# Rooms for down's operands during up, groups of 4, 4, 3 and 3 pairs, and the second norm's plain copy on VectorE, in an encoder step on one Trainium2 core

## The chip, the cores and the metric

The kernel runs on one core of one Trainium2 chip. The metric is the device time of one execution in microseconds (us). The engines are TensorE (PE in the profile; PEld is its weight load), VectorE (DVE), ScalarE (ACT), GpSimd (POOL) and SyncE (SP); SP issues nearly all DMAs here, one after the other, in the order that was fixed when the kernel was built.

## The reference

The reference is one step of a two-layer encoder over 1024 prompt tokens and 32 sample tokens (1056 together), with model width 1024 and hidden width 4096. Layer 0 mixes tokens with an mLSTM, layer 1 with attention over a band of chunks; each is followed by an MLP with a squared ReLU, and each half ends in a layer norm. The change touches the second half of layer 1, and the norm ahead of it:

```
x = layer_norm(ALPHA * x + (1 + g1) * y, ln_g[l, 0], ln_b[l, 0])
u = x * (1 + sc2) + sh2
f = square(relu(u @ w_up[l])) @ w_down[l]
x = layer_norm(ALPHA * x + (1 + g2) * f, ln_g[l, 1], ln_b[l, 1])
```

Everything is float32. A product of matrices is made of three matmuls on operands split into a high and a low part: high by high, high by low, low by high.

## The kernel before

`split` (L88 to L90) makes the two parts of an operand: ACT copies the value into a rounded type (L89, the high part), VectorE subtracts that from the value (L90, the low part). A weight block passes through a landing tile of the tag `raw` (three buffers in a ring pool), is split into a tile of the tag `wc` (six buffers), and is then read by TensorE. Buffers of a tag are handed out in the order in which the program asks for them.

The norm ahead of the MLP (L826 to L891) runs over three token blocks, last one first. For each it subtracts the mean (L844, L857), squares (L859), sums (L844 again), makes the factor (L869 to L874), multiplies (L876), and calls `modulate` (L324) for eight feature chunks and one or two stretches of tokens. `modulate` makes the input u of the MLP: ACT writes its high part (L326), a plain float32 copy of u is made by the engine that is named in the call (here ACT, L330; without a name VectorE, L328), and VectorE subtracts the one from the other (L331). The norm's steps lie between other work by a small planner (`flow`), which advances its generators as matmuls are written.

Layer 1's MLP works on four quarters of 264 tokens (`QN`), and on 16 pairs of 128 hidden features' blocks, 256 features in each. Quarters 3 and 2 are token half 1, quarters 1 and 0 are token half 0, and half 1 comes first. *Up* computes, for a pair and a half, four tiles of 24 matmuls (L118 to L120). For pairs 0 to 13 the four results are squared and combined into seven matrices of a seven-product scheme for blocked multiplication, split, and written to device memory (`hd`, L1468) by groups of pairs (`GRP`: 3, 4, 4 and 3). Pairs 14 and 15 are plain: their squares are split and written to `hpl` (L1473). They are the last of up: pairs 14 and 15 of half 1, then 14 and 15 of half 0.

*Down* then runs over units. A unit is a group and one of four pairs of output blocks; in a unit each token half takes seven products, each of 12 matmuls in a group of 4 pairs and 9 in a group of 3 (L1568). The weights of a unit are two blocks `rdn` (L1518), from which seven combined and split forms `wf` are made by ACT and VectorE (L1535 to L1538, L89, L90) while the unit before runs. The seven operands `fx` of each half are loaded from `hd` (L1551) into fourteen rooms; each is reloaded for the next group as soon as the last unit of the old group has used it. VectorE adds every product to the residual (ACC, L963). The order of the matmuls in down is written out by hand.

The rooms before: one tile of its own (f1), eight in the space that u holds during up (two for each quarter of u), four in a pool (f4) that takes the space of up's combining tiles H and HL after the last pair, and one `wc` tile. The first unit of the first group is split in two, so that output blocks 0 of half 1 and blocks 1 come before blocks 0 of half 0. At the end the plain pairs are read back (`hs`), multiplied with their part of the weights in four token blocks, and the last norm writes the result.

Of the kernel before, what the change touches and what calls it, by code (L numbers as in the profile page):

```python
# [15 lines left out]
P = 128  # L16
# [59 lines left out]
def trunk_kernel(ctx: ExitStack, tc: tile.TileContext, a, o):  # L76
# [744 lines left out]
    def make_layer(acc, pp, uo, usegs=segs):  # L821
# [4 lines left out]
        def norm(ti, ni, nm, w, affine=True, after=None):  # L826
# [48 lines left out]
            for i in range(0, KC, 2):  # L875
                nc.vector.tensor_mul(x[:, i:i + 2], x[:, i:i + 2], w2[:, 0:1].broadcast_to([P, 2, n]))  # L876
                for k in (i, i + 1):
                    for off, m, cnd in usegs(t0, n):
                        tmp = tmp_t([P, 384], f"ut_{nm}_{k}_{off}")
                        modulate(x[:, k, off:off + m], m, comb[:, ni, k, 0, cnd:cnd + 1],  # L880
                                 comb[:, ni, k, 1, cnd:cnd + 1], uo(0, k, t0 + off, m), uo(1, k, t0 + off, m),
                                 tmp[:, :m], nc.scalar)
                if i < 6:
                    yield w[2 + i // 2]
# [175 lines left out]
        return mm, norm, norm_out, out_proj, mlp, gain_shift, add_gated_at  # L1060

# [320 lines left out]

    QN = T // 4
# [41 lines left out]

    NPB, KG = 16, 4
    GRP = [(0, 3), (3, 4), (7, 4), (11, 3)]  # L1430
    NW = 14
    B11, B22, B21, T1, T3, T2, T4 = range(7)
    hd = [[dr.tile([7, P, 2, kg, QN], F32, name=f"hd_{g}_{tp}") for tp in range(2)] for g, (_, kg) in enumerate(GRP)]
    hpl = dr.tile([4, P, 2, T], F32, name="hpl")
    f1_cm = tc.tile_pool(name="f1", bufs=1, reuse_waits="tile")
    f1p = f1_cm.__enter__()
    hh_cm = tc.tile_pool(name="hh", bufs=1, reuse_waits="tile")
    hhp = hh_cm.__enter__()
    w_up, w_dn = a["w_up"][1], a["w_down"][1]
    wups, hts = {}, {}  # L1440

    def up_w(pb):
        if pb not in wups:
            wups[pb] = [wblock(f"up1_{pb}_{i}", w_up, 512 * i, pb * 256) for i in range(2)]
        return wups[pb]

    def up_tile(pb, f, q):

        tp = q // 2
        ps = mm(f"up1_{pb}_{f}_{q}")  # L1450
        proj(ps[:, :QN], QN, up_w(pb), f, lambda hl, k: u2[q][:, hl, k])
        if (pb, tp) not in hts:
            hts[pb, tp] = [hhp.tile([P, 8, QN], F32, tag="H", name=f"H_{pb}_{tp}", bufs=2), 0]
        H = hts[pb, tp][0]
        nc.scalar.activation(H[:, ((0, 1), (3, 2) if pb < NW else (2, 3))[f][q % 2]], ps[:, :QN], AF.Relu)
        hts[pb, tp][1] += 1
        if hts[pb, tp][1] == 4:
            nc.scalar.activation(H[:, 0:4], H[:, 0:4], AF.Square)
            HL = hhp.tile([P, 2, 7, QN], F32R, tag="HL", name=f"HL_{pb}_{tp}", bufs=1)
            if pb < NW:  # L1460
                nc.vector.tensor_sub(H[:, 4:6], H[:, 1:3], H[:, 0:2])
                nc.vector.tensor_sub(H[:, 6], H[:, 2], H[:, 4])
                nc.vector.tensor_sub(H[:, 7], H[:, 3], H[:, 6])
                split(HL[:, 0, 0], HL[:, 1, 0], H[:, 0])
                split(HL[:, 0, 1:], HL[:, 1, 1:], H[:, 2:])
                g = [i for i, (p0, kg) in enumerate(GRP) if p0 <= pb][-1]
                for hl in range(2):
                    nc.sync.dma_start(hd[g][tp][:, :, hl, pb - GRP[g][0]].rearrange("f p t -> p f t"),  # L1468
                                      HL[:, hl].bitcast(F32))
            else:  # L1470
                split(HL[:, 0, 0:4], HL[:, 1, 0:4], H[:, 0:4])
                for c in range(2):
                    nc.sync.dma_start(hpl[2 * (pb - NW) + c, :, :, 2 * tp * QN:2 * (tp + 1) * QN],  # L1473
                                      HL[:, :, 2 * c:2 * c + 2].bitcast(F32).rearrange("p l q t -> p l (q t)"))
        flow.tick(QN / 96)

    def up_unit(pb, tp):
        for f in range(2):
            for q in (2 * tp, 2 * tp + 1):
                up_tile(pb, f, q)  # L1480


    for pb in range(2):
        up_w(pb)
    flow.finish(norms[2])
    for pb in range(2):
        for f in range(2):
            up_tile(pb, f, 3)
    flow.finish(norms[1])
    for pb in range(2):  # L1490
        for f in range(2):
            up_tile(pb, f, 2)
    up_unit(2, 1)
    flow.finish(norms[0])
    for pb in range(3):
        up_unit(pb, 0)
    for pb in range(3, NPB - 2):
        for tp in (1, 0):
            up_unit(pb, tp)
    for tp in (1, 0):  # L1500
        for pb in (NPB - 2, NPB - 1):
            up_unit(pb, tp)

    PRODS = [(0, B11, 0), (1, B21, 1), (2, T2, 0), (3, T1, 2), (4, T3, 0), (5, B22, 2), (6, T4, 0)]
    gate1 = ada_part(1, 5)  # L1510

    def forms(g, m, nm):

        raw = []
        p0, kg = GRP[g]
        for i in range(2):
            r = raw_tile([P, kg, 256], f"rdn_{nm}_{i}")
            nc.sync.dma_start(r, w_dn[p0 * 256:(p0 + kg) * 256, m * 256:(m + 1) * 256].rearrange(  # L1518
                "(k s p) c -> s p k c", s=2, p=P)[i])
            raw.append(r)  # L1520
        out = []

        def pair():
            w = ring.tile([P, 2, 2, kg, P], F32R, tag="wc", name=f"wf_{nm}_{len(out)}", bufs=6)
            out.extend([w[:, 0], w[:, 1]])
            return w
        yield out
        a11, a21 = raw[0][:, :, 0:P], raw[0][:, :, P:256]
        a12, a22 = raw[1][:, :, 0:P], raw[1][:, :, P:256]
        w = pair()  # L1530
        split(w[:, 0, 0], w[:, 0, 1], a11)
        split(w[:, 1, 0], w[:, 1, 1], a12)
        yield out
        s1, s2, s3, s4 = (tmp_t([P, kg, P], f"s{i}_{nm}") for i in range(4))
        nc.vector.tensor_add(s1, a21, a22)  # L1535
        nc.vector.tensor_sub(s2, s1, a11)
        nc.vector.tensor_sub(s3, a11, a21)
        nc.vector.tensor_sub(s4, a12, s2)  # L1538
        for x, y in ((s2, s1), (s3, s4)):
            w = pair()  # L1540
            split(w[:, 0, 0], w[:, 0, 1], x)
            split(w[:, 1, 0], w[:, 1, 1], y)
            yield out
        w = pair()
        split(w[:, 0, 0], w[:, 0, 1], a22)
        yield out

    fx = {}

    def load_f(g, tp, f):  # L1550
        nc.sync.dma_start(fx[tp, f][:, :, :GRP[g][1]].bitcast(F32), hd[g][tp][f])  # L1551

    def unit(g, m, phases, ws, step, after):


        kg = GRP[g][1]
        for tps in phases:
            ps = {}
            for i, (w, f, b) in enumerate(PRODS):
                for tp in tps:  # L1560
                    first = (tp, b) not in ps
                    if first:
                        ps[tp, b] = mm(f"dn1_{g}_{m}_{tp}_{b}")
                    p = ps[tp, b][:, :QN]
                    x = fx[tp, f]
                    for k in range(kg):
                        for n_, (wl, xl) in enumerate(((0, 0), (0, 1), (1, 0))):
                            nc.tensor.matmul(p, ws[w][:, wl, k], x[:, xl, k], start=first and k + n_ == 0,  # L1568
                                             stop=k == kg - 1 and n_ == 2, skip_group_check=not first)
                    c, q = ((0, 0), (0, 0), (0, 1), (1, 1), (1, 1), (0, 1), (1, 0))[i]  # L1570
                    add_gated_at((2 * tp + q) * QN, QN, p, gate1, 2 * m + c)
                    after(tp, f)
                if tps is phases[-1]:
                    step(i)


    def u2_room(q):
        t = u2p[q].tile([P, 2, 2, KG, QN], F32R, tag="u2", name=f"fx_{q}")
        return [t[:, 0], t[:, 1]]
    order_f = [f for _, f, _ in PRODS]  # L1580
    preps, ready = {}, {}
    units = [(0, 0, [(1,)]), (0, 1, [(1,), (0,)]), (0, 0, [(0,)]), (0, 2, [(1, 0)]), (0, 3, [(1,), (0,)])]
    for g in range(1, len(GRP)):
        units += [(g, m, [(1,), (0,)] if m in (0, 3) else [(1, 0)]) for m in range(4)]

    def prep(i):
        if i < len(units):
            preps[i] = forms(*units[i][:2], f"{i}")
            next(preps[i])
    room = u2_room(3) + u2_room(2) + [f1p.tile([P, 2, KG, QN], F32R, name="fx_1")]  # L1590
    for f in order_f[:5]:
        fx[1, f] = room.pop(0)
        load_f(0, 1, f)
    prep(0)
    for _ in range(4):
        ready[0] = next(preps[0])
# [89 lines left out]
```

## Time and profile before

| what | value |
|---|---|
| median of 3 runs | 2502.86 us (2498.45 to 2505.21) |
| profiled execution | 2503.12 us |
| its span, first to last instruction | 2501.3 us |
| mean granted TensorE clock | 0.991 |
| busy: TensorE, VectorE, ScalarE, GpSimd | 2418.5, 1755.0, 1040.4, 167.4 us |
| second norm with the start of up | about 1704 to 1790 us |
| up of layer 1 to its end | to 2113.9 us |
| down by products | 2113.9 to about 2420 us |

The times of the trace are counted from the first instruction of the profiled execution. A row of windows gives from:to, the length, PE's busy time and its number of matmuls, the granted clock (1.00 is full speed), the share in which DMA engines were busy, and GB/s. A row of waits gives the waiting engine, tile and line, what it waited for, the sum in us, how many times, and the longest. A row of groups gives line, engine, operation and shapes, then busy time, mean ns of one, and the idle time ahead of them with what ended it.

### The profile page before, as it was taken

The numbers are of one execution on the slowest core, as the hardware profiler recorded it, in microseconds if no ns is written. First come the engines' busy times: TensorE is split into PE (matmuls) and PEld (weight loads), VectorE is DVE, ScalarE is ACT, GpSimd is POOL, SyncE is SP. The second block draws the span as 40 slices with busy tenths as digits, with TensorE's granted clock in tenths as the row PEclk, the third lists the DMA queues.
The fourth block names the chain that finished last, engine by engine and source line by source line (L and its number), as shares of the span: only waits on it lengthen the run. The fifth ranks groups of instructions, "written<-read, shape, count | busy, mean of one in ns | idle before, by whom it ended". The sixth has DMA issues, their size and how long they took to land.

```text
span 2501.3 us, 42666 instructions
## 1 busy us (share of the span) xinstructions
PE 2418.5 (97%) x16844; PEld 2315.5 (93%) x16844; DVE 1755.0 (70%) x4033; ACT 1040.4 (42%) x2185; POOL 167.4 (7%) x315
## 2 busy tenths in 40 slices
PE   7999999999999999999999899998999999989997
PEld 4999999999999999999999877798999999889997
DVE  4899998778778768766696667737644442766678
ACT  4644455481221221221375566737944443211122
POOL 0211100000000000000001144400000000000003
PEclk9999999999999999999999999999999999999999
DMA  8433234313324323333123400051486667567552
GB/s 295 120 109 100 84 90 132 98 35 118 92 87 126 93 90 121 93 93 115 59 89 94 107 1 2 18 146 43 149 261 209 213 200 247 179 239 285 185 177 70
DMA packets 256108, 316.78 MB, mean 127 GB/s; under 512 B 11160, under 2 KB 233516, under 8 KB 251812
## 3 DMA queue, kind: packets, MB, share of 16 engines
q1 hardware_dynamic: 255908, 314.07, 38.7%
q8 instruction: 132, 2.16, 0.4%
q14 instruction: 68, 0.56, 0.1%
HBM read 241.48 MB, written 74.91 MB: 126 GB/s over the span
## 4 chain that ended last, share of the span: by engine, by line
PE 78%; DVE 7%; DMA 6%; ACT 3%; issue 1%; POOL 0%; SPq 0%; DVEq 0%; ACTq 0%; POOLq 0%
PE up L118 10%; PE up L119 10%; PE up L120 10%; PE dn L1568 8%; PE dn L119 5%; PE dn L118 5%; PE dn L120 5%; PE pv L1308 2%; PE pt L1288 2%; PE s L1258 2%; DMA fx_w<-hd 2%; DMA fx<-hd 1%; PE o L118 1%; PE o L119 1%; PE o L120 1%
## 5 line engine op out<-in xcount | busy, mean ns | idle before, releaser
L1568 PE MATMUL dn<-fx,wf 128*128 128x264 f32 x2184 | 276.7, 286 | 21.0 <-DMA fx<-hd 12.7
L1568 PEld LDWEIGHTS dn<-fx,wf 128*128 128x128 f32 x2184 | 270.4, 190 | 25.8 <-issue 10.9
L119 PE MATMUL up<-u,w_up 128*128 128x264 f32 x1024 | 290.8, 285 | 0.6 <-DVE u L331 0.6
L120 PE MATMUL up<-u,w_up 128*128 128x264 f32 x1024 | 290.0, 285 | 0.0
L118 PE MATMUL up<-u,w_up 128*128 128x264 f32 x1024 | 289.1, 286 | 0.2 <-ACT w_up L89 0.2
L119 PE MATMUL dn<-h,w_dn 128*128 128x384 f32 (+1 forms) x768 | 249.5, 325 | 0.0
L118 PE MATMUL up<-U,w_up 128*128 128x384 f32 (+1 forms) x768 | 249.2, 324 | 0.0
L119 PE MATMUL up<-U,w_up 128*128 128x384 f32 (+1 forms) x768 | 247.9, 323 | 0.0
L118 PE MATMUL dn<-h,w_dn 128*128 128x384 f32 (+1 forms) x768 | 247.8, 323 | 0.0
L120 PE MATMUL up<-U,w_up 128*128 128x384 f32 (+1 forms) x768 | 247.6, 322 | 0.0
L120 PE MATMUL dn<-h,w_dn 128*128 128x384 f32 (+1 forms) x768 | 247.3, 322 | 0.0
L963 DVE SCALAR_TENSOR_TENSOR ACC<-dn,ada,ACC 128x264 f32<-128x264 f32 (+5 forms) x328 | 133.1, 427 | 105.5 <-PE dn L1568 96.6
L119 PEld LDWEIGHTS up<-u,w_up 128*128 128x128 f32 x1024 | 194.5, 190 | 1.1 <-DVE u L331 1.1
L118 PEld LDWEIGHTS up<-u,w_up 128*128 128x128 f32 x1024 | 193.4, 190 | 0.6 <-ACT w_up L89 0.6
L120 PEld LDWEIGHTS up<-u,w_up 128*128 128x128 f32 x1024 | 193.3, 189 | 0.3 <-DVE w_up L90 0.3
L238 DVE SCALAR_TENSOR_TENSOR aacc<-rada,cs,aacc 128x256 f32<-128x256 f32 x448 | 190.3, 477 | 0.0
L963 DVE SCALAR_TENSOR_TENSOR acc<-dn,ada,acc 128x384 f32<-128x384 f32 (+2 forms) x256 | 119.3, 486 | 47.0 <-PE dn L120 45.9
L1000 ACT ACTIVATE r<-up 128x384 f32<-128x384 f32 (+1 forms) x96 | 44.2, 462 | 244.5 <-PE up L120 236.7
L119 PEld LDWEIGHTS dn<-h,w_dn 128*128 128x128 f32 x768 | 144.5, 188 | 0.2 <-DVE h L1003 0.2
L120 PEld LDWEIGHTS dn<-h,w_dn 128*128 128x128 f32 x768 | 144.5, 188 | 0.0
L120 PEld LDWEIGHTS up<-U,w_up 128*128 128x128 f32 x768 | 144.3, 188 | 0.0
L118 PEld LDWEIGHTS up<-U,w_up 128*128 128x128 f32 x768 | 144.2, 188 | 0.1
(350 smaller groups left out, 5986.6 us busy)
## 6 DMA issues: line engine op xcount, KB each, us to landing
hd<-HL SPq DMA_DIRECT2D x56, 924.0 KB
rada<-in_w_ada_dram SPq DMA_DIRECT2D x64, 512.0 KB
raw_up<-in_w_up_dram SPq DMA_DIRECT2D x64, 512.0 KB
fx<-hd SPq DMA_DIRECT2D x26, 1056.0 KB
fx<-hd SPq DMA_DIRECT2D x26, 792.0 KB
raw_dn<-in_w_down_dram SPq DMA_DIRECT2D x36, 512.0 KB
ada_room<-in_w_ada_dram SPq DMA_DIRECT2D x32, 512.0 KB
rada<-in_w_ada_kv_dram SPq DMA_DIRECT2D x16, 512.0 KB
```

Source lines behind the costliest of these rows:

```text
L118: nc.tensor.matmul(ps, wh, mov(0, k), start=(k == 0), stop=False)
L119: nc.tensor.matmul(ps, wh, mov(1, k), start=False, stop=False)
L120: nc.tensor.matmul(ps, wl, mov(0, k), start=False, stop=(k == nk - 1))
L238: nc.vector.scalar_tensor_tensor(acc[:, cnd], raw[:, k], sc, acc[:, cnd], op0=ALU.mult, op1=ALU.add)
L963: nc.vector.scalar_tensor_tensor(xs, ps[:, off + o:off + o + mm_], gate[:, fc, cnd:cnd + 1], xs, op0=ALU.mult, op1=ALU.add)
L1000: nc.scalar.activation(r, ps[:, :n], AF.Relu)
L1258: nc.tensor.matmul(s[:, b, :w], qst, kk[i][:, g, k0 + j0:k0 + j0 + w], start=(i == 0), stop=(i == 1))
L1288: nc.tensor.transpose(pt[:kp, j - j0, pr * P:(pr + 1) * P], ps_[pr][:, j * P:j * P + kp], ident)
L1308: nc.tensor.matmul(pv[64 * e:64 * e + 64, :nq], V[:kp, vt0 + j, g * 64:(g + 1) * 64], pts[e][:kp, j, :nq], start=(j == 0), stop=(j == nt - 1))
L1568: nc.tensor.matmul(p, ws[w][:, wl, k], x[:, xl, k], start=first and k + n_ == 0, stop=k == kg - 1 and n_ == 2, skip_group_check=not first)
```

## The change

The whole of layer 1's MLP moves into a function (`mlp7`) with a small class for what is the layer's own. Beside that:

- The groups are 4, 4, 3 and 3 pairs. The first unit is no longer split, so there are 16 units and not 17.
- The pool of H and HL is closed before the plain pairs, and f4 opens there. The plain pairs get a function of their own, `up_plain`: ACT applies the ReLU into a temporary, VectorE squares it, and it is split into a tile hl, which is taken from the tag `raw` and stored to `hpl`, one store for each feature block and half.
- f1 and the four f4 rooms take the first five operands and are filled before the plain pairs. The rooms in u's quarters 3 and 2 are filled after the plain pairs of half 1, where also the weights of the first unit are requested (`prep(0)`); those in quarters 1 and 0, and the `wc` tile, after the plain pairs of half 0.
- At the end, `hs` takes the f4 tiles, and the last norm's gain and bias take a tile in u's quarter 3.
- In the norm of layer 1 that feeds the MLP, `modulate` is called without an engine, so VectorE makes the plain copy. Layer 0 keeps ACT.

```diff
-                                 tmp[:, :m], nc.scalar)
+                                 tmp[:, :m], nc.scalar if usegs is segs else None)
...
-    GRP = [(0, 3), (3, 4), (7, 4), (11, 3)]
+    GRP = [(0, 4), (4, 4), (8, 3), (11, 3)]
...
+        def up_plain(pb, tp):
+            for f in range(2):
+                r = tmp_t([P, 2, QN], f"hr{l}_{pb}_{f}_{tp}")
+                for i in range(2):
+                    nc.scalar.activation(r[:, i], up_mm(pb, f, 2 * tp + i), AF.Relu)
+                    flow.tick(QN / 96)
+                nc.vector.tensor_mul(r, r, r)
+                hl = ring.tile([P, 2, 2, QN], F32R, tag="raw", name=f"hl{l}_{pb}_{f}_{tp}", bufs=3)
+                split(hl[:, 0], hl[:, 1], r)
+                nc.sync.dma_start(hpl[2 * (pb - NW) + f, :, :, 2 * tp * QN:2 * (tp + 1) * QN],
+                                  hl.bitcast(F32).rearrange("p l q t -> p l (q t)"))
...
+        hh_cm.__exit__(None, None, None)
+        f4_cm = tc.tile_pool(name=f"f4{l}", bufs=1, reuse_waits="tile")
+        f4p = f4_cm.__enter__()
...
-    units = [(0, 0, [(1,)]), (0, 1, [(1,), (0,)]), (0, 0, [(0,)]), (0, 2, [(1, 0)]), (0, 3, [(1,), (0,)])]
-    for g in range(1, len(GRP)):
-        units += [(g, m, [(1,), (0,)] if m in (0, 3) else [(1, 0)]) for m in range(4)]
+        units = [(g, m, [(tp0,), (tp1,)] if m in (0, 3) else [(tp0, tp1)]) for g in range(len(GRP)) for m in range(4)]
...
+        f4 = [f4p.tile([P, 2, KG, QN], F32R, tag=f"f4{i}", name=f"fx_4{i}_{l}") for i in range(4)]
+        rooms = [Room(t) for t in [f1p.tile([P, 2, KG, QN], F32R, name=f"fx_1_{l}")] + f4]
+        want = [(tp, f) for tp in L.pairs for f in order_f]
+
+        def fill(new):
+            for r in new:
+                tp, f = want.pop(0)
+                fx[tp, f] = r
+                load_f(0, tp, f)
+        fill(rooms)
+        for tp in L.pairs:
+            for pb in range(NW, NPB):
+                up_plain(pb, tp)
+            if tp == tp0:
+                fill(L.rooms(tp0))
+                prep(0)
+        for _ in range(4):
+            got[0] = next(preps[0])
+        fill(L.rooms(tp1))
+        fill([Room(ring.tile([P, 2, KG, QN], F32R, tag="wc", name=f"fx_w{l}", bufs=6))])
...
-    hs = [t[:, i] for q in (3, 2) for t in [u2p[q].tile([P, 2, 2, T], F32R, tag="u2", name=f"hs_{q}")] for i in range(2)]
+        hs = [f4p.tile([P, 2, T], F32R, tag=f"f4{c}", name=f"hs_{l}_{c}") for c in range(4)]
...
-    gb = f4p.tile([P, 2, D], F32, tag="f40", name="gb")
+            L1.gb = u2p[3].tile([P, 2, D], F32, tag="u2", name="gb")
```

Here `L.pairs` is (1, 0), so `tp0` is half 1, the half that comes first, and `L.rooms(h)` gives the four rooms in the two quarters of half h.

More of the change, by code (lines that the diff above doesn't have):

```diff
@@ L1060, in make_layer, with __init__, mov, load @@
         return mm, norm, norm_out, out_proj, mlp, gain_shift, add_gated_at
+    QN = T // 4
+    NPB, KG = 16, 4
+    NW = 14
+    GRP = [(0, 4), (4, 4), (8, 3), (11, 3)]
+    B11, B22, B21, T1, T3, T2, T4 = range(7)
+    PRODS = [(0, B11, 0, 0, 0), (1, B21, 1, 0, 0), (2, T2, 0, 0, 1), (3, T1, 2, 1, 1), (4, T3, 0, 1, 1),
+             (5, B22, 2, 0, 1), (6, T4, 0, 1, 0)]
+    class Room:
+        def __init__(self, t, pieces=None):
+            self.t, self.pieces = t, pieces
+        def mov(self, hl, k):
+            return self.t[:, hl, k] if self.pieces is None else self.pieces(hl, k // 2)[:, k % 2 * QN:(k % 2 + 1) * QN]
+        def load(self, src, kg):
+            if self.pieces is None:
+                nc.sync.dma_start(self.t[:, :, :kg].bitcast(F32), src)
+                return
+            for hl in range(2):
+                for k in range(0, kg, 2):
+                    n = min(2, kg - k)
+                    nc.sync.dma_start(self.pieces(hl, k // 2)[:, :n * QN].bitcast(F32),
+                                      src[:, hl, k:k + n].rearrange("p k t -> p (k t)"))
@@ L1381, in trunk_kernel @@
         more_wo(ti)
-    QN = T // 4
     u2_cm, u2p, u2 = [], {}, {}
@@ L1424, in trunk_kernel @@
     out_proj([(0,), (1, 2, 3)], rev, wo_get, o_mov, ada_part(1, 2), end_out1, "b", width=[384, 384, 320])
-    NPB, KG = 16, 4
-    GRP = [(0, 3), (3, 4), (7, 4), (11, 3)]
[L1431 to L1574, printed above, removed]
@@ L1577, in u2_room @@
[L1577 to L1581, printed above, removed]
-    units = [(0, 0, [(1,)]), (0, 1, [(1,), (0,)]), (0, 0, [(0,)]), (0, 2, [(1, 0)]), (0, 3, [(1,), (0,)])]
-    for g in range(1, len(GRP)):
-        units += [(g, m, [(1,), (0,)] if m in (0, 3) else [(1, 0)]) for m in range(4)]
[L1586 to L1596, printed above, removed]
-    hh_cm.__exit__(None, None, None)
-    f4_cm = tc.tile_pool(name="f4", bufs=1, reuse_waits="tile")
-    f4p = f4_cm.__enter__()
-    room = u2_room(1) + u2_room(0) + [f4p.tile([P, 2, KG, QN], F32R, tag=f"f4{i}", name=f"fx_4{i}") for i in range(4)]
-    room.append(ring.tile([P, 2, KG, QN], F32R, tag="wc", name="fx_w", bufs=6))
@@ L1602, in trunk_kernel @@
-    for tp, fs in ((1, order_f[5:]), (0, order_f)):
-        for f in fs:
-            fx[tp, f] = room.pop(0)
-            load_f(0, tp, f)
-    with tc.manual_schedule(engines={mybir.EngineType.PE}):
-        for i, (g, m, phases) in enumerate(units):
-            prep(i + 1)
-            def step(j):
-                if i + 1 in preps and j in (0, 1, 3, 5):
-                    ready[i + 1] = next(preps[i + 1])
-            def after(tp, f):
-                if m == 3 and g + 1 < len(GRP):
-                    load_f(g + 1, tp, f)
-            unit(g, m, phases, ready[i], step, after)
@@ L1620, in trunk_kernel @@
-    hs = [t[:, i] for q in (3, 2) for t in [u2p[q].tile([P, 2, 2, T], F32R, tag="u2", name=f"hs_{q}")] for i in range(2)]
-    for c in range(4):
-        nc.sync.dma_start(hs[c].bitcast(F32), hpl[c])
-    ybuf = [t[:, i] for q in (1, 0) for t in [u2p[q].tile([P, 4, D], F32, tag="u2", name=f"yb_{q}")] for i in range(4)]
-    gb = f4p.tile([P, 2, D], F32, tag="f40", name="gb")
-    nc.sync.dma_start(gb[:, 0], a["ln_g"][1, 1:2].broadcast_to([P, D]))
-    nc.sync.dma_start(gb[:, 1], a["ln_b"][1, 1:2].broadcast_to([P, D]))
@@ L1628, in put_out, with u, ready, rooms @@
-    def put_out(t, m, yr, hf):
-        for off, n, cnd in segs(t, m):
-            dst = o["y_sample"][0] if cnd else o["y_prompt"][0, t:t + n]
-            nc.sync.dma_start(dst[:, 512 * hf:512 * hf + 512], yr[off:off + n, 512 * hf:512 * hf + 512])
-    ws = [wblock(f"dn1_{pr}", w_dn, NW * 256, pr * 256) for pr in range(4)]
-    ny = [0]
-    def next_y(name):
-        ny[0] += 1
-        return ybuf[(ny[0] - 1) % 8]
-    for t0, n in ((0, 288), (288, 256), (544, 256), (800, 256)):
-        for fc in range(KC):
-            ps = mm(f"dn1_{fc}_{t0}")
-            proj(ps[:, :n], n, [ws[fc // 2]], fc % 2, lambda hl, k: hs[k][:, hl, t0:t0 + n])
-            add_gated_at(t0, n, ps, gate1, fc)
-            flow.tick(n / 192)
-        tiles = [(t, min(P, t0 + n - t)) for t in range(t0, t0 + n, P)]
-        flow.add(norm_out(tiles, put_out, next_y, gb, t0 == 800), TAIL[0])
+    class L1:
+        l, alloc, add, gate = 1, mm, add_gated_at, ada_part(1, 5)
+        order, blocks = rev, [(0, 288), (288, 256), (544, 256), (800, 256)]
+        pairs, quarters = (1, 0), (3, 2, 1, 0)
+        def u(hl, k, q):
+            return u2[q][:, hl, k]
+        def ready(i):
+            flow.finish(norms[rev[i]])
+        def rooms(pr):
+            out = []
+            for q in (2 * pr + 1, 2 * pr):
+                t = u2p[q].tile([P, 2, 2, KG, QN], F32R, tag="u2", name=f"fx_{q}")
+                out += [Room(t[:, i]) for i in range(2)]
+            return out
+        def end(f4p):
+            L1.ybuf = [t[:, i] for q in (1, 0) for t in [u2p[q].tile([P, 4, D], F32, tag="u2", name=f"yb_{q}")]
+                       for i in range(4)]
+            L1.gb = u2p[3].tile([P, 2, D], F32, tag="u2", name="gb")
+            nc.sync.dma_start(L1.gb[:, 0], a["ln_g"][1, 1:2].broadcast_to([P, D]))
+            nc.sync.dma_start(L1.gb[:, 1], a["ln_b"][1, 1:2].broadcast_to([P, D]))
+            L1.ny = 0
+        def put_out(t, m, yr, hf):
+            for off, n, cnd in segs(t, m):
+                dst = o["y_sample"][0, t + off - TP:t + off - TP + n] if cnd else o["y_prompt"][0, t:t + n]
+                nc.sync.dma_start(dst[:, 512 * hf:512 * hf + 512], yr[off:off + n, 512 * hf:512 * hf + 512])
+        def next_y(name):
+            L1.ny += 1
+            return L1.ybuf[(L1.ny - 1) % 8]
+        def after(blk):
+            t0, n = blk
+            tiles = [(t, min(P, t0 + n - t)) for t in range(t0, t0 + n, P)]
+            flow.add(norm_out(tiles, L1.put_out, L1.next_y, L1.gb, blk == L1.blocks[-1]), TAIL[0])
@@ L1646, in trunk_kernel @@
+    mlp7(L1)
     flow.finish()
     psD_cm.__exit__(None, None, None)
-    f4_cm.__exit__(None, None, None)
-    f1_cm.__exit__(None, None, None)
     for cm in reversed(u2_cm):
```

145 lines of the change are left out of this document (added).

## The prediction

> **What bounds the kernel now.** I read the page's engine shares first, then windows of layer 1's MLP, then TensorE's waits, then the chain of waits between up and down.
>
> ```profile
> span 2501.3 us, 42666 instructions
> ...
> PE 2418.5 (97%) x16844; PEld 2315.5 (93%) x16844; DVE 1755.0 (70%) x4033; ACT 1040.4 (42%) x2185; POOL 167.4 (7%) x315
> ...
> hd<-HL SPq DMA_DIRECT2D x56, 924.0 KB
> ...
> raw_up<-in_w_up_dram SPq DMA_DIRECT2D x64, 512.0 KB
> fx<-hd SPq DMA_DIRECT2D x26, 1056.0 KB
> fx<-hd SPq DMA_DIRECT2D x26, 792.0 KB
> ```
>
> TensorE (PE) is busy 97% of the span, and the change leaves the number of matmuls as it is. So only stretches in which PE doesn't run at its pace can move the time. Windows of PE (from:to, length, busy and matmuls, granted clock, DMA):
>
> ```profile
> 1728.00:1790.00 62.00, 55.02 (x400) 0.92 0.36 113
> 1790.00:2060.00 270.00, 270.00 (x2236) 1.00 0.68 222
> 2060.00:2113.60 53.60, 53.60 (x445) 1.00 0.61 211
> 2113.60:2160.00 46.40, 36.05 (x258) 0.89 0.61 219
> 2196.00:2240.00 44.00, 35.82 (x277) 1.00 0.64 244
> 2296.00:2310.00 14.00, 11.04 (x85) 1.00 0.89 339
> 2346.00:2350.00 4.00, 4.00 (x35) 1.00 0.32 102
> ```
>
> Undisturbed up runs 2236 matmuls in 270.00 us, 0.1208 us each; a tile of 24 takes 2.90 us, four tiles 11.6. Length less matmuls times 0.1208 is what a window loses: 13.7 us in the second norm (1728 to 1790), nothing in the rest of up, plain pairs included, 15.2 between up and down (2113.6 to 2160), 10.5 where a group of 3 pairs gives way to one of 4 (2196 to 2240), 3.7 from 4 to 4 (2296 to 2310), nothing from 4 to 3 (2346 to 2350).
>
> ```profile
> PE dn L1568 <- DMA fx<-hd: 12.7, 11, 5.1
> ...
> PE mean_n L844 <- ACT sr_n L89: 3.3, 2, 3.2
> PE var_n L844 <- ACT qr_n L89: 3.0, 1, 3.0
> ...
> PE dn L1568 <- DMA fx_w<-hd: 1.9, 2, 0.9
> ```
>
> The largest wait is for fx, down's operands. The chain in order of time (start, length, what):
>
> ```profile
> 2113.76 0.13 PE up L120
> 2113.92 0.40 ACT H L1455
> 2114.34 1.10 ACT H L1458
> 2115.46 1.08 ACT HL L89
> 2116.57 1.26 DVE HL L90
> ...
> 2118.46 0.61 SPq L1473
> 2119.12 7.73 DMA fx<-hd
> ...
> 2126.99 2.33 PE dn L1568 x9
> ...
> 2130.33 7.81 DMA rdn<-in_w_down_dram
> ...
> 2141.93 3.46 DMA rdn<-in_w_down_dram
> ```
>
> Operands that need room freed by up are requested only behind the last plain store, at 2119.12, and PE stands for them. An rdn load (384 KB) issued at 2130.33, behind these loads, lands after 7.81 us; the same load at 2141.93 takes 3.46. SP's loads are served in order, and a late place in its queue is paid in full. By the Trainium skill (DMA: Bandwidth & Descriptors, "Queues, rings and completion order") one sequencer's DMAs share one row of rings, each consumed in ring order; the two rdn rows agree.
>
> **The change part by part.** *Room before the plain pairs: the transition.* Five of the first seven operands are requested before the plain pairs' products, four more after the first half's plain pairs, five after the last. Seven products of 12 matmuls last 84 x 0.1208 = 10.1 us, so unit 0 (both halves) covers 20.3 us of arrivals. After up's end SP still sends five operands (1056 KB), three plain stores and unit 1's two weight blocks of 512 KB.
>
> ```profile
> GB/s 0 288 346 313 181 24 0 349 345 252 0 0 331 218 65 366 398 350 394 278 309 11 119 134 393 91 192 420 341 379 388 242 412 410 401 399 398 376 229 8
> ...
> hpl<-HL SPq DMA_DIRECT2D x8, 528.0 KB
> ```
>
> A backed-up queue moves about 405 GB/s (this is the rate in 2060 to 2140, in 40 slices). Those 7,888 KB take 19.9 us, plus the 2.5 us that the free rdn load took beyond its 0.97 us of data: 22.4, plus a cast and subtraction of some 1.3: 23.7 against 20.3 covered. Remainder about 3 us; of 15.2 are saved 12. If the cover fails, the whole 15.2 comes back.
>
> *Groups 4, 4, 3, 3.* A new group's 14 operands are requested one by one as the 14 products of the old group's last unit end, and read in turn by the 14 of the new one's first. Count from the start of that last unit: products are 1.45 us (12 matmuls) in a group of 4 and 1.09 (9) in one of 3, operands at 405 GB/s (the row of rates below) 2.67 and 2.00, the next units' weights 2.6 and 1.9, and 2.5 us pass in an unhurried load beside its data. From 3 to 4 the 14th lands at 1.09 + 14 x 2.67 + 2.5 + 2.6 = 43.6 and is wanted at 14 x 1.09 + 13 x 1.45 = 34.1: lost 9.5, against 10.5 measured. From 4 to 4: 43.9 and 39.1, lost 4.8 (measured 3.7). From 4 to 3: 33.9 and 34.4, none, as measured. From 3 to 3, which is new: 33.5 and 29.3, lost 4. New sum 3.7 + 0 + 4 = 7.7, old 14.2: saved 6.5. One unit's weight forms fewer lie beside PE; nothing.
>
> *What is put ahead of pair 15's weights.* The plain pairs now write hl tiles of the tag "raw", three buffers, the tag of the weights' landing tiles. In the built order, SP issues raw_up_15 only behind the store of pair 14's second hl tile, and that behind pair 13's last stores, the first hl store and four operand loads; before, pair 15's weights stand ahead of all these, and 2060 to 2113.6 shows no wait. ACT's and VectorE's casts for pair 15 follow the same way.
>
> ```profile
> L1468 SPq DMA_DIRECT2D hd<-HL x2: 360/360/360, 2073.1 to 2075.0; - x2
> ```
> ```profile
> L90 DVE TENSOR_TENSOR w_up<-raw_up,w_up 128x1024 fp32r<-128x1024 f32 x26 | 31.4, 1222 | 21.9 <-ACT w_up L89 21.9
> ...
> L89 ACT CAST w_up<-raw_up 128x1024 fp32r<-128x1024 f32 x26 | 27.2, 1046 | 7.8 <-PE up L120 7.2 <-DMA raw_up<-in_w_up_dram 0.5
> ...
> L1461 DVE TENSOR_TENSOR H<-H 128x528 f32<-128x528 f32 x25 | 17.6, 705 | 42.5 <-ACT H L1458 42.5
> ```
>
> Up ends at 2113.9, 16 tiles after pair 13: call that moment A = 2113.9 - 46.4 = 2067.5. PE wants pair 15 at A + 11.6. Free of any queue: relu 0.40, square 0.71, copy about 0.6 (between nothing and 1.08 for twice the size), subtraction 0.71, store's issue 0.61, so the weights go out near A + 14.7, land 3.8 later (3.46 plus 128 KB more), and cast and subtraction (1.05 + 1.22) end at A + 20.8: PE stands 9.2 us. With the queue: from pair 13's first store (2073.1, A + 5.6) lie ahead 2 x 924, 528, 4 x 1056, 528 and the block's own 512 KB, 7.82 MB, 19.3 us; with 2.5 and the casts A + 29.7: PE stands 18.1. I take the queue's value, since the rows of the transition show this queue in order and backed up. And the clock afterwards:
>
> ```profile
> 2118.50:2127.00 8.50, 2.65 (x19) 0.82 1.00 359
> 2127.00:2134.20 7.20, 6.59 (x28) 0.50 1.03 402
> ```
>
> After the 5 us wait PE had half its clock for about 7 us, 6.59 busy, 3.3 lost. Taken likewise: 18.1 + 3.3 = 21.4. By the Trainium skill (TensorE: Matmul & The Clock Gate, "What's actually happening") a busy window of about 3.4 us brings the clock back, which would lose 1.7; the row here is longer, and I keep 3.3.
>
> The removed squares (one of 1056 on ACT per half pair, now VectorE's) lie beside up's matmuls: nothing.
>
> *The norm's plain copy on VectorE.*
>
> ```profile
> 1704.00:1790.00 86.00, 78.60 (x535) 76.01 (x534) 66.88 (x125) 78.70 (x167) 0.00 (x0) 0.94 0.26 82
> ```
> ```profile
> L330 ACT ACTIVATE ut_n<-ACC,comb 128x240 f32<-128x240 f32 x8 | 4.6, 575 | 0.0
> ...
> L330 ACT ACTIVATE ut_n<-ACC,comb 128x24 f32<-128x24 f32 x8 | 3.1, 392 | 0.0
> ```
> ```profile
> L328 DVE TENSOR_SCALAR utmp<-xt,ada x32: 296/445/480, 36.0 to 63.1; 128x384 f32<-128x384 f32 x16, 128x256 f32<-128x256 f32 x8, 128x32 f32<-128x32 f32 x8
> ```
>
> Busy here, in the order PE, PEld, DVE, ACT: ACT 78.70 of 86, VectorE 66.88. The copies (first and last of seven groups shown) cost ACT 0.39 to 0.58 us each, 56 of them some 27; layer 0's same operation costs VectorE 0.30 to 0.48, at the norm's widths of 24 to 264 some 18 for 56 (an estimate from that row). VectorE would have 85 of 86 us, so the bound changes hands and the stage can't shrink much. Bounds: half of the 13.7 lost gone (the waits for ACT's sr_n and qr_n, 6.3, are its part), or the 18 us pushing the last sums 4 later. I take +1, near the VectorE sum.
>
> *Sum.* 21.4 - 12 - 6.5 + 1 = +3.9 on the profiled 2503.1 (span 2501.3 and 1.8 around it, 0.3 above the median): 2507, less that 0.3. I give 2506.
>
> **Rivals.** *The weights aren't held by the queue* (faster): loads of several requests share the engines, and pair 15's small blocks land in about 3.8 us. For it: in the built order PE interleaves three tiles' first matmuls at pair 15, a short wait for the low halves. Against: the two rdn rows. The wait is then 9.2 and little clock is lost: 2506 - 12 = 2494. It decides once the blocks land before A + 21.
> *The transition keeps its stall* (slower): SP stands until up's end at a load into the last quarters' room, with three stores, four loads and rdn behind it; landings 12 us later than worked out (a slower queue, or hl tiles that wait for their stores) bring the 12 us back: 2518. It decides where unit 1's first block lands later than 25 us after up's end. Against: 20.3 us of cover.
> *ACT's relief shortens the norm* (within the bound): the 6.3 of waits go: 2499. Against: VectorE's 85 of 86. The opposite, VectorE 8 late: 2513.
>
> **How the numbers follow.** A change under 0.3%, 7.5 us, can't be told from none. Forecast 0.46 (2499 to 2513, 0.36 of it within the bound, 0.10 above); weights early 0.20 (0.18 faster, 0.02 within); transition stall kept 0.16, slower; norm shorter 0.10 (0.05 faster with a shorter clock loss, 0.05 within); VectorE late 0.08, slower. Faster 0.23, same 0.43, slower 0.34. Range 2492 (weights early) to 2519 (stall kept).
>
> **What would show it.** Right: a PE wait of some 18 us at pair 15's first tile for w_up and raw_up, with half clock behind it, and SP's raw_up after four fx loads; up's end 20 us later; at most 3 us between up and down, ended by rdn or its forms; losses of about 4 at the first and the third group change; VectorE near full between 1704 and 1790. Wrong: pair 15 starting without a wait, fx waits after up's end, or a norm window that moves by more than 6 us.

## The result, and the profile after

| | before | after |
|---|---|---|
| median of 16 runs | 2503.66 us (2497.53 to 2508.17) | 2509.74 us (2503.0 to 2515.06) |
| profiled execution, its span | 2503.12 us, 2501.3 us | 2513.09 us, 2511.3 us |

The ratio is 1.0027, with a 95% interval of 1.0017 to 1.0036: 6 us slower by the medians, which is under the 0.3% that was named as the limit of what can be told from no change, though the interval excludes 1. The forecast was 2506 us.

The profiled execution of after is 10.0 us longer than that of before, and 3 us above its own median. 2.4 us of this lie ahead of everything that was changed: the norm's first mean starts at 1688.8 in the one and at 1691.2 in the other, before the first plain copy in either (1706.1 and 1708.7), and over the thirteen kernels of this study that moment scatters between 1686.9 and 1691.5. The rest is read from windows that answer to those shown of before (from:to, length, PE busy and matmuls, granted clock, DMA share, GB/s):

```profile
1728.00:1794.00 66.00, 54.71 (x404) 0.95 0.35 111
1794.00:2060.00 266.00, 266.00 (x2202) 1.00 0.66 215
2060.00:2139.50 79.50, 60.85 (x489) 0.89 0.64 226
2139.50:2186.00 46.50, 43.58 (x352) 1.00 0.62 222
2236.00:2250.00 14.00, 11.20 (x88) 1.00 0.96 375
2320.00:2330.00 10.00, 9.64 (x78) 1.00 0.74 261
2380.00:2396.00 16.00, 12.72 (x97) 1.00 0.92 343
2084.20:2102.80 18.60, 0.04 (x1) 0.64 0.94 342
2102.80:2106.80 4.00, 3.91 (x17) 0.53 0.00 0
```

With 0.1208 us to a matmul, as in the prediction, the losses are:

| place | before | after | change |
|---|---|---|---|
| second norm | 13.7 | 17.2 | +3.5 |
| plain pairs, to up's end | 0 | 20.4 | +20.4 |
| behind up's end | 15.2 | 4.0 | -11.2 |
| group changes | 10.5 + 3.7 + 0 | 3.4 + 0.6 + 4.3 | -5.9 |
| sum | | | +6.8 |

Two rows depend on where their windows begin and end. The norm's windows both begin at 1728, where the profiled execution of after is 2.4 us late; counted from the same matmul to the same matmul (the norm's first mean to the 401st of up, 102.0 and 104.8 us) the norm takes 2.8 us more. A group change also loses a little outside the short windows. Counted from the start of the old group's last unit to the end of the new group's second, the three changes lose 11.3, 4.0 and 0.8 us before and 3.8, 1.6 and 5.7 after, 5.0 less; the last of them, from 3 pairs to 3, is

```profile
2358.18:2409.93 51.75, 47.95 (x381) 1.00 0.72 266
```

So one new wait of 18.6 us with 2 us of half clock behind it takes back what the earlier operands (11) and the new groups (5 to 6) gained, and the norm adds to it. TensorE's waits from 1500 us on show the same exchange. The wait for ACT's w_up was 0.2 us before, the wait for fx was 12.7:

```profile
PE up L118 <- ACT w_up L89: 18.6, 1, 18.6
PE var_n L844 <- ACT qr_n L89: 7.0, 2, 3.9
PE dn L1238 <- DMA fx<-hd: 4.3, 6, 0.9
PE mean_n L844 <- ACT sr_n L89: 3.5, 1, 3.5
...
PE dn L1238 <- DVE ACC L963: 3.4, 5, 1.1
```

The chain of waits at pair 15, in order of time (start, length, what), is the path that the prediction named link by link, with the queue as its longest link:

```profile
2084.28 0.40 ACT hr L1154
2084.68 0.02 issue
2084.70 0.72 DVE hr L1156
2085.42 0.02 issue
2085.44 0.64 ACT hl L89
2086.08 0.02 issue
2086.11 0.72 DVE hl L90
2086.82 0.02 issue
2086.84 0.56 SPq L1159
2087.39 0.04 issue
2087.44 14.33 DMA raw_up<-in_w_up_dram
2101.77 0.02 issue
2101.79 1.05 ACT w_up L89
2102.85 0.04 issue
2102.89 0.59 PE up L118
```

512 KB take 14.33 us from issue to landing, where the 384 KB of a free load took 3.46 in the trace of before.

### The profile page after: what moved, and what is told of

Its sections match the earlier page's. It is cut to its first block, busy times and chain, and to the rows that moved or that the text cites. A ratio compares the mean times of both kernels' runs of the same rounds, so it can differ in the third digit from the quotient of the medians.

```text
span 2511.3 us, 42707 instructions
## 1 busy us (share of the span) xinstructions
PE 2420.0 (96%) x16844; PEld 2317.1 (92%) x16844; DVE 1769.5 (70%) x4090; ACT 1016.6 (40%) x2122; POOL 167.9 (7%) x315
## 4 chain that ended last, share of the span: by engine, by line
PE 76%; DVE 9%; DMA 7%; ACT 3%; issue 1%; POOL 0%; SPq 0%; DVEq 0%; ACTq 0%; POOLq 0%
PE up L118 9%; PE up L119 9%; PE up L120 9%; PE dn L1238 7%; PE dn L119 5%; PE dn L118 5%; PE dn L120 5%; PE pv L1549 2%; DMA fx_w<-hd 2%; PE pt L1529 2%; PE s L1499 2%; PE o L118 1%; PE o L119 1%; PE o L120 1%; PE op_b L118 1%
## 5 line engine op out<-in xcount | busy, mean ns | idle before, releaser
L118 PE MATMUL up<-u,w_up 128*128 128x264 f32 x1024 | 290.5, 286 | 19.5 <-ACT w_up L89 18.6
L1238 PEld LDWEIGHTS dn<-fx,wf 128*128 128x128 f32 x2184 | 267.2, 188 | 12.7 <-issue 5.0
L963 DVE SCALAR_TENSOR_TENSOR ACC<-dn,ada,ACC 128x264 f32<-128x264 f32 (+4 forms) x328 | 133.4, 427 | 85.2 <-PE dn L1238 76.3
L120 PEld LDWEIGHTS up<-U,w_up 128*128 128x128 f32 x768 | 144.3, 188 | 0.0
L118 PEld LDWEIGHTS up<-U,w_up 128*128 128x128 f32 x768 | 144.2, 188 | 0.1
L119 PEld LDWEIGHTS up<-U,w_up 128*128 128x128 f32 x768 | 144.2, 188 | 0.0
```

What stands on the lines that cost most here:

```text
L118: nc.tensor.matmul(ps, wh, mov(0, k), start=(k == 0), stop=False)
L119: nc.tensor.matmul(ps, wh, mov(1, k), start=False, stop=False)
L120: nc.tensor.matmul(ps, wl, mov(0, k), start=False, stop=(k == nk - 1))
L963: nc.vector.scalar_tensor_tensor(xs, ps[:, off + o:off + o + mm_], gate[:, fc, cnd:cnd + 1], xs, op0=ALU.mult, op1=ALU.add)
L1238: nc.tensor.matmul(p, ws[w][:, wl, k], x.mov(xl, k), start=first and k + n_ == 0, stop=k == kg - 1 and n_ == 2, skip_group_check=not first)
```

## The experiments

The theory was that the shared tag `raw` puts pair 15's weights behind pair 14's stores and four operand loads in SP's queue; that this queue is served in order, so that what lies ahead sets the wait; and that VectorE's new work costs the norm a few us. Each experiment changes one thing of the changed kernel or of the one before, unless it says otherwise.

### Pair 15's weights asked for early

```diff
+        for pb in range(NW, NPB):
+            up_w(pb)
         fill(rooms)
```

> The changed kernel, with the weights of pairs 14 and 15 asked for ahead of the operand loads and the plain pairs; nothing else differs. If the 18.6 us wait of TensorE comes from pair 15's weights standing behind pair 14's hl stores and four operand loads in SP's queue, it goes, and with it the half clock behind it (1.9 us): 20 us less than the changed kernel, about 2489 us, some 14 less than before. Rival: the wait only moves, because the operand loads then share the engines with something TensorE needs as much; then less than 8 us are gained and a new wait of over 10 us stands at pair 15 or after up's end.

Median 2498.04 us, ratio to before 0.9969 (0.9958 to 0.998): 11.7 us less than the changed kernel. The wait at pair 15 is gone altogether, so its cause is the late request. But 6 of the 20 us come back at another place. The rival had named a wait after up's end, but one of over 10 us: TensorE stands 5.0 us there, at the third product of unit 0.

```profile
2119.70:2166.00 46.30, 39.88 (x303) 0.93 0.66 233
```

That window loses 46.3 - 303 x 0.1208 = 9.7 us, where the changed kernel loses 4.0. The profile finds nothing that ended the 5.0 us ("issue"), but the code and the times do. The first and the third product of a unit add into the same accumulator tile (their `b` in `PRODS` is 0), and VectorE's ACC of the first product reads that tile between the two. Here this ACC stands on VectorE behind unit 0's weight forms. Of this kernel, the first of the forms, that ACC and the third product (start, length, what):

```profile
2117.94 0.62 ACT L89 CAST wf<-rdn 128x512 fp32r<-128x512 f32 x1
2128.34 0.48 DVE L963 SCALAR_TENSOR_TENSOR ACC<-dn,ada,ACC 128x264 f32<-128x264 f32 x1
2128.92 18.70 PE L1238 MATMUL dn<-fx,wf 128*128 128x264 f32 x132 [5.03 <-issue]
```

The product starts 0.10 us after the ACC ends; in the eight kernels of this study in which it has to wait there, it starts 0.10 or 0.11 us after. The forms are late because their weights are. In both kernels the weights are asked for 17 or 18 us before unit 0 starts. Here that is at 2102.7, and the first form starts 15.2 us later, 1.9 us before unit 0. In the changed kernel it is at 2121.4, and the first form starts 10.3 us later, 7.8 us before unit 0:

```profile
2131.74 0.62 ACT L89 CAST wf<-rdn 128x512 fp32r<-128x512 f32 x1 [0.29 <-DMA rdn<-in_w_down_dram]
```

What the wait at pair 15 had given was time for the queue to empty: nothing moves between 2102.8 and 2106.8 in the changed kernel, while here the DMA engines are busy throughout from 2083 to 2102.7 (a share of 1.01), and the weights find that queue ahead of them.

### Three of the four loads moved behind the weights

```diff
-        fill(rooms)
+        fill(rooms[:1])
         for tp in L.pairs:
             for pb in range(NW, NPB):
                 up_plain(pb, tp)
+                if tp == tp0 and pb == NW:
+                    up_w(NW + 1)
+                    fill(rooms[1:])
```

> The changed kernel, with pair 15's weights still behind pair 14's second hl store, but with only one of the four f4 operand loads ahead of them; the other three come after. Theory of the queue: three loads of 1056 KB at 405 GB/s are 8 us, so the wait at pair 15 falls from 18.6 to about 11 us. Theory that the chain through hl (multiply, copy, subtract, store) sets the wait: it stays at 17 or more. Theory that loads share the engines rather than queue: it was near 9 already and can't fall by more than 1 or 2.

One run, without repeated timing, 2501.60 us: the wait is 9.8 us and not 18.6. The weights are still asked for behind pair 14's second store, and the chain through hl is unchanged, but the load is quicker:

```profile
PE up L118 <- ACT w_up L89: 9.8, 1, 9.8
```
```profile
2084.31 5.47 DMA raw_up<-in_w_up_dram
```

5.47 us with one operand load of the four ahead, 14.33 with all four: 8.9 us for three loads of 1056 KB, some 365 GB/s. This decides between queue and chain, and against loads that share the engines side by side. It also bounds the two parts of the 18.6 us: about half is the chain and a load with little ahead of it, half the queue. Behind the wait TensorE has half its clock for longer than in the changed kernel:

```profile
2090.90:2096.50 5.60, 5.60 (x25) 0.50 1.01 413
```

### hl in another tag

```diff
-                hl = ring.tile([P, 2, 2, QN], F32R, tag="raw", name=f"hl{l}_{pb}_{f}_{tp}", bufs=3)
+                hl = ring.tile([P, 2, 2, QN], F32R, tag="wc", name=f"hl{l}_{pb}_{f}_{tp}", bufs=6)
```

> The changed kernel, with the plain pairs' hl tiles from the tag of the split weights (wc, six buffers) instead of the landing tiles' (raw, three); program order is untouched. If the shared tag raw is what puts pair 15's weights late, TensorE's wait at pair 15 goes as in the run with the weights asked for early: about 2489 us. If the order in which the program asks is the cause by itself, the wait stays near 18 us and the time at 2510.

Median 2493.55 us, ratio 0.9962 (0.9948 to 0.9977). With the order of the program untouched, the wait at pair 15 falls to 2.8 us, so the tag is the cause: buffers of a tag are given out in the program's order, and pair 15's landing tiles came behind pair 14's hl tiles. (Whether more buffers in `raw` would have done the same was not tried.) A wait of 2.8 us there and one of 2.4 us for the forms behind up's end remain. The first is no longer the load's: SP asks for the last of pair 15's weights at 2024.5, but ACT copies them only behind pair 14's second hl tile, from 2083.3.

```profile
PE up L118 <- ACT w_up L89: 2.8, 1, 2.8
PE dn L1238 <- ACT wf L89: 2.4, 1, 2.4
```

### The norm's copy back on ACT

```diff
-                                 tmp[:, :m], nc.scalar if usegs is segs else None)
+                                 tmp[:, :m], nc.scalar)
```

> The changed kernel, with the second norm's plain copy back on ACT; nothing else differs. Theory: VectorE became the bound of the norm, and the new 3.1 us wait for qr_n at block 0's variance is its price; the norm loses about 3 us less: 2507 us, and VectorE's busy time between 1704 and 1790 falls back by 13. Rival: the copy on VectorE cost nothing, and the time stays within 1 us of the changed kernel's.

Median 2508.92 us, ratio to before 1.0024 (1.0015 to 1.0033), against 1.0027 (1.0017 to 1.0036) of the changed kernel: 0.8 us less by the medians, which the two intervals don't tell apart. The wait at block 0's variance is gone, as expected: 2.9 us in one wait remain of 7.0 in two, and VectorE's busy time between 1704 and 1790 falls from 79.69 to 66.80 us.

### The norm's copy on VectorE, in the kernel before

The same line in the kernel before, the other way round.

> The kernel before, with only the second norm's plain copy moved to VectorE. Theory that VectorE becomes the norm's bound: a wait of about 3 us for qr_n at block 0's variance appears and the norm loses 2 to 3 us more: 2506, ratio about 1.001. Rival: nothing, within 1 us of before.

Median 2507.22 us against 2503.85, ratio 1.0013 (1.0002 to 1.0024): 3 us slower by the medians, with an interval that only just leaves 1 out. TensorE's waits and the busy times of the norm (PE, PEld, DVE, ACT in this order), of this kernel:

```profile
PE var_n L844 <- ACT qr_n L89: 7.0, 2, 3.8
PE mean_n L844 <- ACT sr_n L89: 2.5, 1, 2.5
PE up L118 <- ACT u L326: 1.0, 1, 1.0
```
```profile
1704.00:1790.00 86.00, 76.20 (x512) 74.45 (x512) 79.07 (x178) 62.62 (x120) 0.00 (x0) 0.94 0.26 82
```

ACT falls from 78.70 to 62.62, VectorE rises from 66.88 to 79.07. The two runs agree on the mechanism (the second wait for qr_n comes and goes with the copy). On the size their times say little: 0.8 and 3.4 us by the medians, with intervals that reach from nothing to 6 us. The profiled executions say more, since the other edits of this study act later in the program. From the norm's first mean to the 401st matmul of up, the seven kernels with the copy on ACT take 102.0 to 103.5 us, the six with it on VectorE 104.4 to 105.8: by the means 2.1 us more.

### Only the groups, in the kernel before

```diff
-    GRP = [(0, 3), (3, 4), (7, 4), (11, 3)]
+    GRP = [(0, 4), (4, 4), (8, 3), (11, 3)]
```

> The kernel before, with only the groups of 4, 4, 3 and 3 pairs (first unit still split, rooms as before). The two group changes that are left with a loss cost some 8 us and not 14, as in the changed kernel: 6 less. Theory that the rooms are needed for the larger first group: the wait between up and down grows, because its operands are 1056 KB and not 792, 14 of them, of which nine are asked for late: some 5 to 8 us more there, so the time stays at 2501 to 2506. Rival: the transition is unchanged at 15 us, and the time is 2497.

Median 2500.94 us, ratio 0.9989 (0.998 to 0.9998): 3 us less. Behind up's end TensorE's waits come together in one:

```profile
PE dn L1568 <- DVE ACC L963: 13.8, 4, 11.6
```
```profile
2115.80:2162.00 46.20, 32.52 (x249) 0.89 0.67 260
```

The window loses 16.1 us, 0.9 more than before, but ends before the losses of the first units do. From up's end to the start of the first group's last unit, this kernel and the kernel before show

```profile
2115.89:2194.78 78.89, 64.16 (x507) 0.94 0.48 179
```
```profile
2113.72:2175.03 61.31, 50.96 (x381) 0.92 0.52 183
```

They lose 17.6 and 15.3 us, so the larger first group costs the old transition 2.4 us, less than the 5 to 8 that were expected. The group changes, counted over whole units as above, lose 4.2, 0.8 and 6.2 us, 5.0 less than before. Together that is 2.6 us gained, about what the time shows: the groups gain by themselves, without the new rooms.

### The old groups, in the changed kernel

The edit of the run before, the other way round.

> The changed kernel, with the old groups of 3, 4, 4 and 3 pairs. The change from 3 to 4 comes back with a loss of about 10 us, the one from 3 to 3 (4.6) goes, so the group changes cost 5 us more; the wait at pair 15 falls by about 2.5, because the four operand loads ahead of its weights are 792 KB each (4 x 0.67 us less data); together about 2512. If the loads' size doesn't matter to that wait, 2515.

Median 2515.42 us, ratio 1.0044 (1.0028 to 1.0059): 5.7 us more than the changed kernel; 2512 was expected. The wait at pair 15 falls to 15.6 us, by 3.0 where 2.5 were worked out from the smaller loads ahead, and the change from 3 to 4 costs

```profile
2190.00:2250.00 60.00, 51.99 (x410) 1.00 0.75 294
```

60 - 410 x 0.1208 = 10.5 us again. Not expected was a wait of 2.9 us early in unit 0: it is the third product again, 0.10 us behind the first product's ACC.

### Early weights, the norm on ACT, and the forms earlier in the program

The edits of the first and the fourth experiment together, and

```diff
             for pb in range(NW, NPB):
                 up_plain(pb, tp)
+                if tp == tp1 and pb == NW:
+                    for _ in range(4):
+                        got[0] = next(preps[0])
             if tp == tp0:
                 fill(L.rooms(tp0))
                 prep(0)
-        for _ in range(4):
-            got[0] = next(preps[0])
```

> The changed kernel, with pair 15's weights asked for early, the norm's copy on ACT, and unit 0's weight forms written between the two plain pairs of the second half. The early weights alone left a new wait of 5.0 us (8.8 lost with the half clock) after up's end, where the forms of unit 0 came late on ACT and VectorE, behind the plain pairs' ReLUs; with them earlier it goes, to 2 us at most, and the norm gives 2.5: about 2488 us, ratio 0.994. If that wait was the operands' and not the forms', it stays: about 2495.

Median 2490.88 us, ratio 0.9955 (0.9938 to 0.9971). The time is near the one expected, but the wait stayed: 4.8 us after up's end. The forms are now ahead in ACT's order and ACT stands for their weights:

```profile
ACT wf L89 <- DMA rdn<-in_w_down_dram: 9.3, 2, 8.5
```
```profile
2097.50 15.60 DMA rdn<-in_w_down_dram
```

Unit 0's second block is issued at 2097.50 behind four operand loads and lands 15.60 us later: the same queue once more, at the next place. The third product then starts at 2121.66, 0.11 us after the first product's ACC, which stands on VectorE behind the late forms and two of the plain pairs' squares.

### Unit 0's blocks ahead of the four loads

```diff
             if tp == tp0:
-                fill(L.rooms(tp0))
                 prep(0)
+                fill(L.rooms(tp0))
```

> The kernel of the last run, with unit 0's weight blocks asked for ahead of the four operand loads into quarters 3 and 2, not behind them. In that run ACT waited 8.5 us for the first block, which was issued at 2096.8 and landed near 2111.7, and TensorE then stood 4.8 us at its third product. Theory of the queue: four loads of 1056 KB less ahead are 10.7 us, the forms are ready before up ends, and the wait after up's end goes (7.4 lost there, at most 2 left): about 2485, ratio 0.993. Rival: the operands that now come 2.6 us later are missed in their place, and the time stays near 2491.

Median 2490.52 us, ratio 0.9948 (0.9934 to 0.9961). The wait of 4.8 us is gone, and the time is the same within the intervals: the rival came true in its effect. Waits for operands took its place.

```profile
PE dn L1238 <- DMA fx<-hd: 2.0, 3, 0.9
PE dn L1238 <- DVE ACC L963: 1.2, 2, 0.8
PE dn L1238 <- DMA fx_w<-hd: 1.0, 1, 1.0
```
```profile
2115.40:2162.00 46.60, 41.70 (x330) 1.00 0.60 214
```

Here the window loses 6.7 us. In this kernel's order SP puts all loads into quarters 1 and 0 behind the last plain store, so they are asked for only after up's end.

### The same with hl in the tag wc

> As the run before, with the hl tiles in the tag wc too. Unit 0's blocks then stand ahead of all of the plain pairs' stores and loads. If the queue is all that made them late, both reach the same time, about 2485; if the tag wc makes unit 1's forms wait for hl's buffers, a wait of 2 us or more stands at unit 1 and it is slower than the run before.

Median 2485.03 us, ratio 0.9928 (0.9911 to 0.9946), the fastest of the study by the medians: 17.7 us less than before in the same comparison, and 24.7 less than the change's median. Against the run before it is 5.5 us less by the medians, which neither expectation had, and the two intervals overlap. Unit 0's blocks go out ahead of all of the plain pairs' transfers. Behind up's end

```profile
2112.70:2160.00 47.30, 44.92 (x365) 1.00 0.56 197
```

3.2 us are lost, and nothing from 2060 to 2112.7 (438 matmuls in 52.70 us). No wait for forms stands at unit 1; the longest wait there is 1.3 us, for ACC.

### The forms behind the plain pairs again

The edit of "Unit 0's blocks ahead of the four loads" without the moved forms.

> As the first of these three, but with the forms of unit 0 written behind the second half's plain pairs, as in the changed kernel. Theory that the place of the blocks in SP's queue is what matters: the wait after up's end is gone here too, 2 us at most. Theory that the forms' place in ACT's and VectorE's order matters: a wait of 4 to 6 us stands after up's end, as with the early weights alone.

One run, without repeated timing, 2490.41 us; the wait after up's end is 2.8 us. It lies between the two theories: the blocks' place in SP's queue and the forms' place in ACT's and VectorE's order both have a part, and this run doesn't part them further. Here too the third product starts 0.11 us after the first product's ACC, which on VectorE comes behind the forms and two subtractions for hl.

## Why the prediction was right

The time came out 3.7 us above the forecast by the medians of this comparison, and within its range. By its steps:

- *Pair 15's weights* (the queue's value, 18.1 us): 18.6 measured. Each link stands in the chain: 0.40, 0.72, 0.64 (0.6 taken), 0.72, 0.56. The rival that the weights come early because loads share the engines falls by the second experiment, and the tag as the cause is shown by the third.
- *The clock behind it* (3.3 us): 17 matmuls in 4.00 us at 0.53 of the clock, 1.9 lost. This term was too large. The row that it was taken from had waits within the stretch. By the Trainium skill (TensorE: Matmul & The Clock Gate, "What's actually happening") a busy window of about 3.4 us brings the clock back, which makes an estimate of 1.7; this row is near it. The second experiment is not: 25 matmuls in 5.60 us at 0.50, 2.6 lost.
- *The transition* (12 saved, some 3 left): 11.2 saved, 4.0 left. That it came so near is in part luck. It rests on a cover that the prediction hadn't named: the wait at pair 15 let the queue empty before unit 0's weights were asked for, and without that wait 9.7 are lost, as the first experiment shows.
- *Groups* (3.7, 0 and 4 left, 6.5 saved): 3.4, 0.6 and 4.3, 5.9 saved; over whole units 5.0 saved, with 5.7 left at the change from 3 to 3.
- *The norm* (+1, bounds of half of 13.7 gained and 4 lost): 3.5 more in the window, 2.8 from matmul to matmul, 2.1 by the means of all kernels. The sign was right and the term too small. VectorE's 18 us of copies were 20 (its groups run from 0.29 to 0.41 us each), its busy time came to 79.69 of 86 and not to 85, and the price was one more wait of 3.1 us for block 0's qr_n, which the sum of busy times doesn't show.

By the table of losses the queue, the transition, the groups and the norm came out 0.5, 0.8, 0.6 and 2.5 us dearer than forecast, and the clock 1.4 cheaper, which helped the sum to come near: 6.8 against 3.9. The rival of a transition that keeps its stall didn't come true; the longest wait behind up's end was 1.2 us. The profile puts it down to hl's copy on ACT, but it is the third product of unit 0, which starts at 2143.80, 0.10 us after the first product's ACC.

## What to carry to other kernels

A tile that is written late and stored from a ring of landing tiles can hold back the loads that come after it in that ring, even one that nothing else delays, as pair 15's weights here; look at where a ring's next request stands in the built order, not in the program. With one in-order queue for all transfers, price a load by the bytes ahead of it, and put small blocks that a bound engine waits for ahead of the large ones that are needed later. When a long wait is removed, look at what had rested on it: here the queue had emptied during the wait, and without it first the weight forms (and the ACC behind them), then the operands came late. The best time came when the queue's order was mended for all three. And where a product waits although its operands are there, look at what still reads the tile that it writes.

## What the runs showed that was not expected

- Moving a block ahead of four loads removed a wait of 4.8 us and gave nothing (2490.88 and 2490.52 us), because SP's order put other loads later in exchange.
- The stretch of half clock does not grow with the wait ahead of it: 4.0 us behind 18.6 us without work, 5.6 us behind 9.8 us (the second experiment), 7.2 us behind 5.1 us in the kernel before, with short waits inside.
- The groups alone, without the rooms, gain 3 us (0.9989), although the first group's operands are a third larger and were expected to cost the transition as much; there they cost 2.4 us.
